# Weight sums of the seven-product feed-forward input: GpSimd additions replaced by accumulating DMAs, with all sums turned to pure sums

## The chip, the cores and the metric

The kernel runs on one core of a Trainium2 chip. The core has a matrix engine (TensorE, PE in the profile), a vector engine (VectorE, DVE), a scalar engine (ScalarE, ACT), a general engine (GpSimd, POOL) and a queue engine (SyncE, SP), each with its own instruction stream, and 16 DMA engines that serve all queues. The metric is the device time of one execution in microseconds; lower is better. Times given are medians of several runs; the profile is of one further execution.

## What is computed

A two-layer transformer-like backbone over 512 latent tokens of width 1024 with 256 context tokens, all in float32. Layer 0 mixes tokens by windowed attention, layer 1 by a gated chunk mixer; each is followed by a gated feed-forward block, and it is the input half of that block that this case is about:

```python
def swiglu(h, w_in, w_out):
    gate, up = jnp.split(h @ w_in, 2, axis=-1)
    return (jax.nn.silu(gate) * up) @ w_out
...
        x = x + g_ml * rmsnorm(y_l, norm_g[i, 1])
        f_l = swiglu(modulate(rmsnorm(x, norm_g[i, 2]), sh_fl, sc_fl), ffn_w_in[i], ffn_w_out[i])
        x = x + g_fl * rmsnorm(f_l, norm_g[i, 3])
```

Here `h` is 512 x 1024, `w_in` is 1024 x 5632 and `w_out` 2816 x 1024.

## The kernel before

**Precision.** Every float32 matrix product is made of three products of reduced-precision parts: each operand is split into a high part (a cast on ScalarE, `high`, line 217) and a low part (the operand minus its high part on VectorE, `low`, line 220), and TensorE adds high x high, high x low and low x high (`mm3`, `product`).

**The weight stream.** All weights lie in DRAM as 88 units of 128 partitions x 2048 floats (1 MB). `Stream.fetch` loads one into one of two `w_raw` buffers with a DMA issued on SP's queue. SP runs ahead of the compute engines and is held only by the semaphores of what it overwrites.

**The feed-forward input.** For layer 0 the units are 10 to 31 (`u0 = 10`), for layer 1 they are 55 to 76; unit n of a layer (n = 0 to 21) has 128 gate columns and the 128 matching up columns. Units 0 and 1 are done in the plain way (`head`). Units 2 to 21 are done by a Winograd form of Strassen's scheme: activations and weights are cut in 2 x 2 quarters (activations: half of the 1024 inputs by half of the 512 tokens; weights: half of the inputs by gate or up, B11, B12, B21, B22) and the four quarter results come from seven quarter products instead of eight. The price is sums of quarters:

- on the activation side S1 to S4, made once per layer on VectorE (`first_half`, `sum_a`), and split into high and low parts (`sum_high`, `sum_low`);
- on the weight side, for every unit, T1 = B12 - B11, T3 = B22 - B12, T2 = T3 + B11, T4 = B21 - T2. They are made by four GpSimd instructions (`diff`, line 1389) out of the raw unit into a tile named T of 128 x 2048 floats, from a pool named `big` with two buffers. The order in the tile is T1, T2, T3, T4, 512 floats each.

`part_high` and `part_low` then split four things per unit: B11 (tile `x`), T1 with T2 (part 1, `w_hi` and `w_lo` from T), the raw second half B21 with B22 (part 2, from `w_raw`), and T3 with T4 (part 3, from T). `product(n, i)` does one of the seven products: 4 slices x 3 matmuls of 128 x 128 by 256 columns (line 1432). Products 5 and 6 read part 1, products 2 and 3 part 2, products 7 and 4 part 3; product 4 of a unit is done in the step of the next unit. `keep`, `up1`, `up2` and `gate1` on ScalarE and VectorE combine the quarter results out of PSUM, `silu` and `gates` finish the activations.

**What sets the order.** `rest` (line 1495 on) writes a plan: `at(time, step, ...)` notes a step with a planned time, T = 10.08 us per unit, with b the start of a unit. `run_plan` issues the steps sorted: a step whose name stands in the list `ORDER` goes by its rank there, any other by its planned time behind them. The order on each engine's queue is the order of issue; the times themselves are not kept on the chip, where an instruction starts when its engine reaches it and its semaphores are there. In the plan `diff` of unit n + 1 stands at b + 0.02 to b + 3.9, its four `part_high` at b + 2.1, 5, 6.6 and 8.9, and the fetch of unit n + 2 at b + 9.1. `prepare` plans the first sums of a layer (unit 2) inside the end of the stage before, beside `head` and the activation sums.

Beside this the loop loads one modulation row of the next stage in 512 KB chunks on SP's queue (`fetch_chunk`, 8 per layer), adds them up on VectorE (`add_chunk`), and clears its accumulator once per layer with a memset on POOL (`Ada.start`, line 351).

Of the kernel before, what the change touches and what calls it, by code (L numbers as in the profile page):

```python
# [11 lines left out]
ALU = mybir.AluOpType  # L12
# [4 lines left out]
KC = D // P  # L17
# [141 lines left out]
f0sum_high_S1 f0head_3_1 wfetch_13 f0part_low_2_2 f0sum_low_S2 f0head_3_2 f0sum_low_S1 f0sum_high_S3 f0part_low_2_1  # L159
# [39 lines left out]
f1head_3_1 f1sum_high_S3 wfetch_58 f1sum_high_S1 f1head_3_2 f1sum_low_S1 f1sum_low_S2 f1part_low_2_3 f1sum_low_S3  # L199
# [4 lines left out]
def backbone_kernel(ctx: ExitStack, tc: tile.TileContext, a, out):  # L204
    nc = tc.nc
# [7 lines left out]
    def dma(dst, src):  # L213
        nc.sync.dma_start(out=dst, in_=src)
# [36 lines left out]
    def big(name):  # L251
        return base.tile([P, 2 * D], F32, name=name, tag="big", bufs=2)
# [1018 lines left out]
    class FFN:  # L1271
# [77 lines left out]
        def sum_a(self, name, c):  # L1349

            if c.t == 2 and name in ("S3", "S2"):
                self.sums[name] = self.sum_tile(vec if name == "S3" else stage32)
            s1, s2, s3, s4 = (self.sums[n][:, :, (c.t - 2) * P:(c.t - 1) * P] if n in self.sums else None
                              for n in ("S1", "S2", "S3", "S4"))
            a21, a22 = (c.pt[:, z * 512:(z + 1) * 512].rearrange("p (k s) -> p k s", k=4) for z in range(2))
            out, in0, in1, op = {"S3": (s3, s1, a21, ALU.subtract), "S2": (s2, a22, s3, ALU.subtract),
                                 "S1": (s1, s2, s1, ALU.add), "S4": (s4, s4, s2, ALU.subtract)}[name]
            nc.vector.tensor_tensor(out=out, in0=in0, in1=in1, op=op)
# [21 lines left out]

        def diff(self, n, i):
            if i == 1:
                self.T[n] = big("T")
            T = {j: self.T[n][:, o * 512:(o + 1) * 512].rearrange("p (k m) -> p k m", k=4)
                 for j, o in ((1, 0), (2, 1), (3, 2), (4, 3))}
            q = lambda b: self.quarter(n, b)
            x, y, op = {1: lambda: (q("B12"), q("B11"), ALU.subtract), 3: lambda: (q("B22"), q("B12"), ALU.subtract),
                        2: lambda: (T[3], q("B11"), ALU.add), 4: lambda: (q("B21"), T[2], ALU.subtract)}[i]()
            nc.gpsimd.tensor_tensor(out=T[i], in0=x, in1=y, op=op)  # L1389
# [51 lines left out]
        def up2(self, n):  # L1441
            c = self.c[n]
            nc.vector.tensor_tensor(out=c[:, 768:], in0=self.ps[n, 0], in1=c[:, 256:512], op=ALU.add)  # L1443
# [17 lines left out]
        def prepare(self, ch):  # L1461
# [29 lines left out]
        def rest(self, nxt_of, head, **kw):  # L1491
# [3 lines left out]
            for n in range(2, NFF):  # L1495
# [353 lines left out]
```

## Time and profile before

| what | value |
|---|---|
| median of 3 runs | 1141.66 us (1139.63 to 1144.7) |
| profiled execution, span from first to last instruction | 1138.5 us |
| TensorE busy | 1121.0 us, 98% |
| VectorE busy | 879.6 us, 77% |
| ScalarE busy | 565.4 us, 50% |
| POOL busy | 488.3 us, 43% |
| DMA queue of SP | 157.04 MB, 37.6% of the 16 engines' span |
| feed-forward input loops | about 304 to 505 and 808 to 1010 us |

The page gives the span of the profiled execution only; the timed runs are other executions and contain what lies ahead of the first and behind the last instruction. In the rows, a group is given as line, engine, operation, output <- inputs, count, busy time in us, mean ns of one, and the idle time of the engine just ahead of it with what ended that idle time. In a list of windows the columns are the window, its length, busy time (and number of instructions) of PE, PEld, DVE, ACT and POOL, the granted TensorE clock, the busy share of the DMA engines and GB/s. Matmuls are pipelined, so one matmul's own duration is longer than the distance from it to the next.

### The profile page before, as it was taken

To read this page: it belongs to the slowest core of one execution; us is meant where nothing else is said; L and a number is where in the kernel's file an instruction comes from. 1 tells how busy PE (TensorE), PEld (TensorE's weight loads), DVE (VectorE), ACT (ScalarE), POOL (GpSimd) and SP (SyncE) were. 2 spreads that over 40 slices of the span, in tenths; PEclk is the share of its full clock that TensorE was granted. 3 is DMA by queue.
4 is the path that set the end of the run, shared out by engine and by line. 5 is a ranking of instruction groups with operands and counts; after the bars stand their busy time and mean duration, and the time that the engine had idled before them with its cause. 6 is when DMAs were issued, how large, how long until landed. Compare 5 with 4: busy or idle time off the path is not lost.

```text
span 1138.5 us, 18345 instructions
## 1 busy us (share of the span) xinstructions
PE 1121.0 (98%) x7358; PEld 998.8 (88%) x7358; DVE 879.6 (77%) x1140; ACT 565.4 (50%) x983; POOL 488.3 (43%) x341
## 2 busy tenths in 40 slices
PE   8999999999999999999999999999999999999997
PEld 5789887768999999998888888888999999998886
DVE  6688988958988989889865768747989899953325
ACT  6357768656554455543324545345545555533322
POOL 2357475515677767730001313006577676700000
PEclk9999999999999999999999999999999999999999
DMA  9732232233134233368753265331142333323221
GB/s 370 278 137 103 102 112 75 75 148 111 57 131 149 95 136 140 130 222 320 290 185 111 87 216 194 111 114 39 66 176 96 136 140 130 130 90 133 75 74 74
DMA packets 25881, 158.21 MB, mean 139 GB/s; under 512 B 3386, under 2 KB 3642, under 8 KB 9540
## 3 DMA queue, kind: packets, MB, share of 16 engines
q1 hardware_dynamic: 25796, 157.04, 37.6%
q8 instruction: 57, 0.93, 0.3%
q14 instruction: 28, 0.23, 0.1%
HBM read 154.94 MB, written 2.10 MB: 138 GB/s over the span
## 4 chain that ended last, share of the span: by engine, by line
PE 87%; DVE 6%; DMA 2%; issue 2%; ACT 2%; POOL 0%; SPq 0%; DVEq 0%; POOLq 0%; ACTq 0%
PE f L1432 33%; PE y L272 27%; PE v L272 3%; PE o_ps L931 2%; PE pT_ps L911 2%; DMA ada<-in_ada 2%; PE s_ps L877 1%; PE u L1674 1%; PE u L1676 1%; PE u L1675 1%; PE s_ps L878 1%; PE q_ps L264 1%; PE q_ps L266 1%; PE q_ps L265 1%; DVE w_lo L220 1%
## 5 line engine op out<-in xcount | busy, mean ns | idle before, releaser
L272 PE MATMUL y<-w_hi,st 128*128 128x512 f32 x928 | 251.4, 389 | 0.0
L220 DVE TENSOR_TENSOR w_lo<-w_raw,w_hi 128x1024 fp32r<-128x1024 f32 (+1 forms) x109 | 151.5, 1391 | 100.6 <-ACT w_hi L217 100.6
L217 ACT CAST w_hi<-w_raw 128x1024 fp32r<-128x1024 f32 x122 | 127.8, 1052 | 179.1 <-PE y L272 123.7
L272 PEld LDWEIGHTS y<-w_hi,st 128*128 128x128 f32 x928 | 173.8, 188 | 36.1
L1389 POOL TENSOR_TENSOR T<-w_raw 128x512 f32<-128x512 f32 x80 | 139.1, 1759 | 111.2 <-DMA w_raw<-in_w 79.3
L1432 PE MATMUL f<-H,w_hi 128*128 128x256 f32 x960 | 178.2, 283 | 2.5 <-DVE fc L1443 2.5
L1432 PEld LDWEIGHTS f<-H,w_hi 128*128 128x128 f32 x960 | 150.1, 192 | 3.4 <-DVE fc L1443 2.9
L245 POOL TENSOR_TENSOR ry<-ry,mhalf 128x1 f32<-128x1 f32 x16 | 9.2, 576 | 327.1 <-DVE ry L242 164.2
L220 DVE TENSOR_TENSOR w_lo<-T,w_hi 128x1024 fp32r<-128x1024 f32 x80 | 143.4, 1793 | 4.4 <-ACT w_hi L217 4.4
L272 PE MATMUL y<-w_lo,st 128*128 128x512 f32 x464 | 144.2, 389 | 0.0
L1432 PE MATMUL f<-H,w_lo 128*128 128x256 f32 x480 | 135.7, 283 | 0.0
L1432 PE MATMUL f<-S,w_hi 128*128 128x256 f32 x640 | 120.0, 285 | 0.3 <-ACT fc L1439 0.3
L217 ACT CAST w_hi<-T 128x1024 fp32r<-128x1024 f32 x80 | 83.6, 1046 | 55.0 <-PE f L1432 29.7
L1439 ACT COPY fc<-f 128x256 f32<-128x256 f32 x120 | 44.8, 373 | 122.5 <-PE f L1432 120.0
L272 PEld LDWEIGHTS y<-w_lo,st 128*128 128x128 f32 x464 | 87.0, 188 | 18.0
L1432 PEld LDWEIGHTS f<-S,w_hi 128*128 128x128 f32 x640 | 99.5, 192 | 0.9 <-ACT fc L1439 0.5
L360 DVE SCALAR_TENSOR_TENSOR acc<-ada_raw,sc,acc 128x1024 f32<-128x1024 f32 x64 | 84.9, 1326 | 10.8 <-DMA ada_raw<-in_ada 8.1
L1432 PEld LDWEIGHTS f<-H,w_lo 128*128 128x128 f32 x480 | 92.1, 192 | 0.0
L1432 PE MATMUL f<-S,w_lo 128*128 128x256 f32 x320 | 90.7, 284 | 0.5 <-DVE w_lo L220 0.5
L1389 POOL TENSOR_TENSOR T<-w_raw,T 128x512 f32<-128x512 f32 x40 | 82.8, 2070 | 3.1
L905 POOL TENSOR_SCALAR p<-p,st 128x512 f32<-128x512 f32 (+1 forms) x64 | 55.7, 885 | 44.3 <-DVE st L901 21.6
L1389 POOL TENSOR_TENSOR T<-T,w_raw 128x512 f32<-128x512 f32 x40 | 69.0, 1726 | 3.1
(238 smaller groups left out, 2524.4 us busy)
## 6 DMA issues: line engine op xcount, KB each, us to landing
w_raw<-in_w SPq DMA_DIRECT2D x87, 1024.0 KB, 4.9
ada_raw<-in_ada SPq DMA_DIRECT2D x32, 1024.0 KB, 6.1
ada<-in_ada SPq DMA_DIRECT2D x8, 1024.0 KB, 9.4
ada_k<-in_ada SPq DMA_DIRECT2D x16, 512.0 KB, 5.7
row<-in_norm_g SPq DMA_DIRECT2D x7, 512.0 KB, 5.5
xin<-in_x SPq DMA_DIRECT2D x4, 512.0 KB, 7.6
x<-in_x SPq DMA_DIRECT2D x4, 512.0 KB, 6.2
out<-x SPq DMA_DIRECT2D x3, 512.0 KB, 2.6
```

Of the source, the lines that this page charges most:

```text
L217: nc.scalar.copy(out=hi, in_=src)
L220: (eng or nc.vector).tensor_tensor(out=lo, in0=src, in1=hi.bitcast(F32), op=ALU.subtract)
L264: nc.tensor.matmul(dst, lh, rh, start=first, stop=False)
L265: nc.tensor.matmul(dst, lh, rl, start=False, stop=False)
L272: nc.tensor.matmul(dst, l, w[:, n * 512:(n + 1) * 512], start=first and i == 0, stop=last and i == 2)
L360: nc.vector.scalar_tensor_tensor(out=ac, in0=w, scalar=sc[:, k:k + 1], in1=ac, op0=ALU.mult, op1=ALU.add)
L905: nc.gpsimd.tensor_scalar(out=p, in0=p, scalar1=self.st[:, 12 + j:13 + j], scalar2=1.0, op0=ALU.mult, op1=ALU.mult)
L911: nc.tensor.transpose(ps[:, j * P:(j + 1) * P], self.probs[j][:, i * P:(i + 1) * P], ident)
L931: nc.tensor.matmul(self.o[z * HD:(z + 1) * HD, c], v, pt[:, c], start=i < 2, stop=i >= self.nb - 2, tile_position=(0, z * HD), skip_group_ ...
L1389: nc.gpsimd.tensor_tensor(out=T[i], in0=x, in1=y, op=op)
L1432: nc.tensor.matmul(dst, l[:, w], r[:, k, :], start=first and k == 0 and j == 0, stop=k == 3 and j == 2, skip_group_check=True)
L1439: nc.scalar.copy(out=self.c[n][:, i * 256:(i + 1) * 256], in_=self.ps[n, 1 if i == 1 else 0])
```

## The change

The four weight sums of units 3 to 21 of both layers are no longer made by `diff`. In their place:

- `sums_start(n)` takes the T tile and issues four plain loads from DRAM on SP's queue, quarter by quarter: T1 <- B12, T2 <- B11, T3 <- B12, T4 <- B21. A quarter has rows of 128 floats (512 bytes) in DRAM. It is planned two units ahead, at b + 1.2; for unit 3 it stands in `ORDER` behind the fetch of unit 3.
- `sums_add(n, i)` issues DMAs on POOL's queue that add to what is there: for i = 0 T1 += B11 and T3 += B22 from DRAM, for i = 1 T2 += T3, for i = 2 T4 += T2, the latter two from SBUF to SBUF. Each is cut into two halves of 64 partitions, so a unit has 4 + 2 + 2 of them, 128 KB each. They are planned one unit ahead, at b - 6, b - 3.5 and b - 1.
- Signs: all four weight sums are now sums (T1 = B12 + B11, T3 = B22 + B12, T2 = T3 + B11, T4 = B21 + T2). To match, S2 and S4 change sign on VectorE (S2 by one two-operation instruction in place of a subtraction), and `up2` and `up1` subtract the product.
- `diff` remains for unit 2 of each layer, with additions.

The raw fetch of every unit remains, for B11 and for B21 with B22.

```diff
             a21, a22 = (c.pt[:, z * 512:(z + 1) * 512].rearrange("p (k s) -> p k s", k=4) for z in range(2))
-            out, in0, in1, op = {"S3": (s3, s1, a21, ALU.subtract), "S2": (s2, a22, s3, ALU.subtract),
-                                 "S1": (s1, s2, s1, ALU.add), "S4": (s4, s4, s2, ALU.subtract)}[name]
+            if name == "S2":
+                nc.vector.scalar_tensor_tensor(out=s2, in0=s3, scalar=-1.0, in1=a22, op0=ALU.mult, op1=ALU.subtract)
+                return
+            out, in0, in1, op = {"S3": (s3, s1, a21, ALU.subtract), "S1": (s1, s2, s1, ALU.add),
+                                 "S4": (s4, s4, s2, ALU.add)}[name]
             nc.vector.tensor_tensor(out=out, in0=in0, in1=in1, op=op)
...
+        def sums_start(self, n):
+
+            T, w = self.new_T(n), a["w"][self.u0 + n].rearrange("p (k z m) -> p k z m", k=KC, z=2)
+            for j, k, z in ((1, 0, 1), (2, 0, 0), (3, 0, 1), (4, 4, 0)):
+                dma(T[j], w[:, k:k + 4, z, :])
+
+        def sums_add(self, n, i):
+
+            T, w = self.t_parts(n), a["w"][self.u0 + n].rearrange("p (k z m) -> p k z m", k=KC, z=2)
+            flat = {j: self.T[n][:, (j - 1) * 512:j * 512] for j in (2, 3, 4)}
+            for h in range(2):
+                p = slice(64 * h, 64 * h + 64)
+                if i == 0:
+                    nc.gpsimd.dma_start(out=T[1][p], in_=w[p, 0:4, 0, :], accum_op=ALU.add)
+                    nc.gpsimd.dma_start(out=T[3][p], in_=w[p, 4:, 1, :], accum_op=ALU.add)
+                else:
+                    j = 2 * i
+                    nc.gpsimd.dma_start(out=flat[j][p], in_=flat[{2: 3, 4: 2}[j]][p], accum_op=ALU.add)
...
         def diff(self, n, i):
...
-            x, y, op = {1: lambda: (q("B12"), q("B11"), ALU.subtract), 3: lambda: (q("B22"), q("B12"), ALU.subtract),
-                        2: lambda: (T[3], q("B11"), ALU.add), 4: lambda: (q("B21"), T[2], ALU.subtract)}[i]()
-            nc.gpsimd.tensor_tensor(out=T[i], in0=x, in1=y, op=op)
+            x, y = {1: lambda: (q("B12"), q("B11")), 3: lambda: (q("B22"), q("B12")),
+                    2: lambda: (T[3], q("B11")), 4: lambda: (q("B21"), T[2])}[i]()
+            nc.gpsimd.tensor_tensor(out=T[i], in0=x, in1=y, op=ALU.add)
...
-            nc.vector.tensor_tensor(out=c[:, 768:], in0=self.ps[n, 0], in1=c[:, 256:512], op=ALU.add)
+            nc.vector.tensor_tensor(out=c[:, 768:], in0=c[:, 256:512], in1=self.ps[n, 0], op=ALU.subtract)
...
-            nc.vector.tensor_tensor(out=c, in0=self.ps[n, 1], in1=c, op=ALU.add)
+            nc.vector.tensor_tensor(out=c, in0=self.ps[n, 1], in1=c, op=ALU.subtract)
...
+            at(33, self.sums_start, 3)
...
                 if n < last:
-                    for i, j in enumerate((1, 3, 2, 4)):
-                        at(b + .02 + 1.28 * i, self.diff, n + 1, j)
+                    for i in range(3):
+                        at(b - 6 + 2.5 * i, self.sums_add, n + 1, i)
...
                 at(b + 9.1, ws.fetch, u0 + n + 2 if n < last - 1 else f2 + n - last + 1)
+                if n < last - 1:
+                    at(b + 1.2, self.sums_start, n + 2)
```

More of the change, by code (lines that the diff above doesn't have):

```diff
@@ L158 @@
 f0sum_a_S3#2 f0sum_a_S1 f0sum_a_S2#2 f0sum_a_S4#2 f0head_2_2 f0head_3_0 f0sum_high_S4 f0sum_a_S1#2 f0sum_high_S2
-f0sum_high_S1 f0head_3_1 wfetch_13 f0part_low_2_2 f0sum_low_S2 f0head_3_2 f0sum_low_S1 f0sum_high_S3 f0part_low_2_1
+f0sum_high_S1 f0head_3_1 wfetch_13 f0sums_start_3 f0part_low_2_2 f0sum_low_S2 f0head_3_2 f0sum_low_S1 f0sum_high_S3 f0part_low_2_1
 f0sum_low_S4 f0part_low_2_3 f0sum_low_S3 whigh_43_0 work_9_0 work_10_0 wlow_43_0 c0square_y#2 whigh_43_1 c0gain_y#2
@@ L198 @@
 f1part_high_2_3 f1head_2_2 f1sum_high_S4 f1sum_a_S1#2 f1part_low_2_1 f1head_3_0 f1sum_low_S4 f1part_low_2_2
-f1head_3_1 f1sum_high_S3 wfetch_58 f1sum_high_S1 f1head_3_2 f1sum_low_S1 f1sum_low_S2 f1part_low_2_3 f1sum_low_S3
+f1head_3_1 f1sum_high_S3 wfetch_58 f1sums_start_3 f1sum_high_S1 f1head_3_2 f1sum_low_S1 f1sum_low_S2 f1part_low_2_3 f1sum_low_S3
 """.split()
@@ L1379, in quarter, with new_T, t_parts @@
             return ws.raws[self.u0 + n].rearrange("p (k z m) -> p k z m", k=KC, z=2)[:, 4 * i:4 * i + 4, z, :]
+        def sums_start(self, n):
[13 more added lines that the diff above has]
+                    nc.gpsimd.dma_start(out=flat[j][p], in_=flat[{2: 3, 4: 2}[j]][p], accum_op=ALU.add)
+        def new_T(self, n):
+            self.T[n] = big("T")
+            return self.t_parts(n)
+        def t_parts(self, n):
+            return {j: self.T[n][:, o * 512:(o + 1) * 512].rearrange("p (k m) -> p k m", k=4)
+                    for j, o in ((1, 0), (2, 1), (3, 2), (4, 3))}
         def diff(self, n, i):
             if i == 1:
-                self.T[n] = big("T")
-            T = {j: self.T[n][:, o * 512:(o + 1) * 512].rearrange("p (k m) -> p k m", k=4)
-                 for j, o in ((1, 0), (2, 1), (3, 2), (4, 3))}
+                self.new_T(n)
+            T = self.t_parts(n)
             q = lambda b: self.quarter(n, b)
-            x, y, op = {1: lambda: (q("B12"), q("B11"), ALU.subtract), 3: lambda: (q("B22"), q("B12"), ALU.subtract),
-                        2: lambda: (T[3], q("B11"), ALU.add), 4: lambda: (q("B21"), T[2], ALU.subtract)}[i]()
-            nc.gpsimd.tensor_tensor(out=T[i], in0=x, in1=y, op=op)
+            x, y = {1: lambda: (q("B12"), q("B11")), 3: lambda: (q("B22"), q("B12")),
+                    2: lambda: (T[3], q("B11")), 4: lambda: (q("B21"), T[2])}[i]()
+            nc.gpsimd.tensor_tensor(out=T[i], in0=x, in1=y, op=ALU.add)
         def source(self, n, i):
```

## The prediction

> **What bounds the kernel now.** I read the head of the page, then the chain that ended last in order of time, then the busy time of windows inside the two feed-forward loops, then who waited for whom on TensorE.
>
> ```profile
> span 1138.5 us, 18345 instructions
> PE 1121.0 (98%) x7358; PEld 998.8 (88%) x7358; DVE 879.6 (77%) x1140; ACT 565.4 (50%) x983; POOL 488.3 (43%) x341
> L1389 POOL TENSOR_TENSOR T<-w_raw 128x512 f32<-128x512 f32 x80 | 139.1, 1759 | 111.2 <-DMA w_raw<-in_w 79.3
> L1389 POOL TENSOR_TENSOR T<-w_raw,T 128x512 f32<-128x512 f32 x40 | 82.8, 2070 | 3.1
> L1389 POOL TENSOR_TENSOR T<-T,w_raw 128x512 f32<-128x512 f32 x40 | 69.0, 1726 | 3.1
> L220 DVE TENSOR_TENSOR w_lo<-T,w_hi 128x1024 fp32r<-128x1024 f32 x80 | 143.4, 1793 | 4.4 <-ACT w_hi L217 4.4
> ```
> ```profile
> 316.80 172.80 PE f L1432 x1428
> 821.39 174.50 PE f L1432 x1452
> ```
> ```profile
> 384.00:424.00 40.00, 40.00 (x333) 39.91 (x332) 35.99 (x35) 20.24 (x36) 29.08 (x17) 1.00 0.36 132
> 888.00:928.00 40.00, 40.00 (x336) 40.00 (x335) 37.16 (x35) 20.82 (x36) 28.98 (x17) 1.00 0.37 133
> ```
> ```profile
> PE f L1432 <- DVE fc L1443: 1.4, 1, 1.4
> PE f L1432 <- DVE w_lo L220: 0.5, 1, 0.5
> ...
> PE f L1432 <- ACT fc L1439: 0.3, 1, 0.3
> ...
> PE f L1432 <- DVE fc L1443: 1.1, 1, 1.1
> PE fa L266 <- DVE H L220: 0.9, 1, 0.9
> ```
>
> The second fence is the chain: start, length, what. In the second layer 1452 matmuls of the seven products stand in a row in 174.50 us, 120.2 ns each, with nothing between them. A step (one column block, 84 matmuls: 7 products, 4 slices, 3 matmuls) therefore takes 84 x 0.1202 = 10.1 us (I use the planner's 10.08). The windows (columns: PE, PEld, DVE, ACT, POOL busy, clock, DMA share, GB/s) say the same: TensorE busy 40.00 of 40.00 at clock 1.00. The POOL work that the change removes is 139.1 + 82.8 + 69.0 = 290.9 us, but its finished sums are never what the last fence names: those are all of TensorE's waits from 264 to 330, 480 to 530 and 780 to 830 us, 1.4 + 0.5 + 0.3 + 1.1 + 0.9 = 4.2 us. So **the most that a perfect cover could gain is about 4.2 us**, 0.4%.
>
> **What goes away, and its price.** Of 160 POOL sums, the 8 for unit 2 of each layer are split 4 and 4 and stay; 152 go, 38 units' worth. Removing them shortens no chain by itself. It also frees VectorE: the low part of the T halves takes 1793 ns in the mean beside POOL and 1.23 us in the row of 380.72 below, so about 0.56 us x 76 = 43 us of VectorE, hidden under TensorE but for the 4.2 us. The turned signs (four sums per token block and the two `up` steps on VectorE) keep one instruction for one of the same size: nothing, and less than 1 us per layer if the cover were gone, since they are some dozen instructions.
>
> **What is added, per unit.** On SP's queue 4 plain loads of 256 KB in 512-byte rows (1.05 MB), behind a wait until the T buffer of two units earlier is read. On POOL's queue 8 accumulating DMAs of 128 KB: four (T1 += B11, T3 += B22, each in two partition halves), then two that wait for T3, then two that wait for T2. POOL now computes nothing here, but its queue is in order, and each wait holds what follows.
>
> ```profile
> 379.64 1.04 ACT L217 CAST w_hi<-T 128x1024 fp32r<-128x1024 f32 x1
> 383.72 1.05 ACT L217 CAST w_hi<-T 128x1024 fp32r<-128x1024 f32 x1 [1.51 <-PE f L1432]
> 380.72 1.23 DVE L220 TENSOR_TENSOR w_lo<-T,w_hi 128x1024 fp32r<-128x1024 f32 x1 [0.24 <-ACT w_hi L217]
> 382.67 1.52 DVE L220 TENSOR_TENSOR w_lo<-w_raw,w_hi 128x1024 fp32r<-128x1024 f32 x1
> 387.71 2.31 DVE L220 TENSOR_TENSOR w_lo<-T,w_hi 128x1024 fp32r<-128x1024 f32 x1
> 390.10 3.38 POOL L1389 TENSOR_TENSOR T<-w_raw 128x512 f32<-128x512 f32 x2 [1.16 <-DVE w_lo L220]
> 395.80 2.16 POOL L1389 TENSOR_TENSOR T<-w_raw,T 128x512 f32<-128x512 f32 x1
> 386.44 0.40 PE L1432 MATMUL f<-S,w_hi 128*128 128x256 f32 x2
> 393.72 0.40 PE L1432 MATMUL f<-H,w_hi 128*128 128x256 f32 x2
> 388.35 0.62 ACT L217 CAST x<-w_raw 128x512 fp32r<-128x512 f32 x1
> 384.25 0.33 SPq L214 DMA_DIRECT2D w_raw<-in_w  x1
> ```
> ```profile
> w_raw<-in_w SPq DMA_DIRECT2D x87, 1024.0 KB, 4.9
> out<-x SPq DMA_DIRECT2D x3, 512.0 KB, 2.6
> cc<-in_cc SPq DMA_DIRECT2D x1, 8.0 KB, 1.8
> L351 POOL MEMSET acc<- 128x1024 f32 x10 | 9.5, 955 | 15.5 <-PE f L1432 15.5
> ```
>
> No accumulating DMA and no DMA issued from POOL is in this trace, so two costs are bounded from rows. **Issue on POOL, g:** at least the 0.33 us that SP takes to issue a load, at most POOL's 2.16 us for one sum. I take 0.95 us, the memset: like the writing of descriptors it reads no operand. **Landing, L:** at least the 1.8 us of the 8 KB load, at most the 4.9 us of a 1 MB one. The rate comes from the windows: 132 GB/s at share 0.36 is about 365 GB/s at full share. An accumulating DMA of 131 KB must read both its operand and its destination, 0.262 MB, 0.72 us; another queue's loads run beside it for much of the step, so I double that: L = 1.8 + 1.44 = 3.24 us.
>
> From these, three limits on a step:
>
> (a) *POOL's queue.* The halves overlap: four issues (4g), T3's second half lands (L), its T2 issue (g), lands (L), its T4 issue (g). The round is 6g + 2L = 5.7 + 6.5 = **12.2 us**. Ends: 6 x 0.33 + 2 x 1.8 = 5.6 and 6 x 2.16 + 2 x 4.9 = 22.8.
>
> (b) *The 16 DMA engines.* Now 0.36 x 10.08 = 3.63 us of a step; the loads add 1.05 MB / 365 = 2.87; the adds 2.10 MB / 365 = 5.75 with both reads, half of it if the second read costs nothing. Sum **12.25 us**, or 9.4. If the 512-byte rows go at half the rate (unshown), the loads cost 5.75 and the adds 2.87 + 5.75 = 8.62, in all 18.0.
> In the Trainium skill, "Collectives: The Full Stack", section "The bandwidth ceiling: the fold count and why AG ≠ RS ≠ AR", an add in the DMA engines runs at half a copy's rate because of the second source read. By it the 12.25 stands and the 9.4 falls; no row here shows an add, so I keep both.
>
> (c) *The two T buffers.* T is free when its second low part ends, 387.71 + 2.31 = 390.02. The load of the unit two later lands 4.9 later (w_raw's row, same bytes), T4 after 6g + 3L = 15.4, cast and low part take 1.05 + 1.23: 22.6 us per two steps, 11.3 a step. SP is held there too: the raw fetch, issued now at 384.25 when the raw low part is done (382.67 + 1.52), comes behind the wait, after 390.02 and four issues of 0.33, 391.3. Both loads, 2.1 MB, take 5.75 + 1.8 and land near 398.0 to 398.9; the cast that reads the fetch comes one step after 388.35, at 398.4. Just covered; if not, 0.5 us once per layer. Behind that wait on SP stands one 512 KB chunk of the next modulation row every second step, and behind POOL's waits only the next unit's adds and one memset per layer.
>
> **Where the stall lands.** The first late T: the T12 half of the unit is cast two steps after 379.64, at 399.8. Now T2 is ready by 395.80, where POOL goes on to T4, 4 us ahead. With the change T2 lands 390.02 + 4.9 + (5g + 2L = 11.2) = 406.1, 6.3 late. Its low part ends now at 380.72 + 1.23 = 381.95 and TensorE reads it at 386.44: 4.5 us in hand. The T34 half is cast two steps after 383.72, at 403.9, and T4 lands at 390.02 + 4.9 + 15.4 = 410.3, 6.4 late, with 393.72 - 390.02 = 3.7 in hand. ScalarE is blocked in order meanwhile, and the copies that free PSUM are queued behind it, so what isn't in hand reaches TensorE: about 3 us the first time. After that the slack is spent and each step costs the excess of the slowest limit, 12.25 - 10.08 = 2.17 us.
>
> **Sum.** Units 4 to 21 of a layer: 3 + 17 x 2.17 = 39.9; two layers 79.8. Span 1138.5 + 79.8 = 1218.3. The page gives only the profiled span; the median of the runs, 1141.66, lies 3.2 above it. 1218.3 + 3.2 = **1221 us**, 7% slower.
>
> **Rivals.** *Hidden* (25%): g near SP's 0.33 and adds at copy rate give 5.6, 9.4 and (4.9 + 6 x 0.33 + 3 x 1.8 + 2.28) / 2 = 7.3 us, all within 10.08. Then 1141.7 less at most 4.2: 1137.5 to 1141.7. For it: every cost is unmeasured, and POOL's 43% becomes nearly idle. Against it: at the middle values all three limits come out above the step.
>
> *The adds land without a fight* (12%): L is the 2.6 us of the 512 KB store, the round 5.7 + 5.2 = 10.9; 3 + 17 x 0.82 = 17 per layer, 1176 us. It needs the second read to be cheap too.
> In the Trainium skill, "DMA: Bandwidth & Descriptors", section "Anatomy of one DMA — SWDGE (gpsimd) path", such a DMA takes 2.0 us plus its bytes at 436 GB/s, estimated 2.6 us for 0.26 MB, which is this case.
>
> *The halves don't overlap* (17%): if the waits are on the whole T tile, the round is 8g + 2L = 14.1, 4.0 over; 3 + 17 x 4.0 = 71, 1284 us. That the steps name disjoint partitions speaks against it.
>
> *Short rows halve the DMA rate* (7%): 18.0 us, 3 + 17 x 7.9 = 137 per layer, 1416 us.
>
> *Faster beyond the cover* (3%): VectorE's freed 43 us would have to shorten TensorE by more than 5.7 us, and its waits are 4.2.
>
> *That the change doesn't move the work:* POOL keeps the queue of all the sums, so it can stay the pacing engine while shown as idle; that is limit (a).
>
> **Chances.** 36% for the forecast, the others as given. A change of this kernel can be told from none beyond about 0.5%, 5.7 us (the three runs span 5.1). Slower: 36 + 12 + 17 + 7 = 72%; within: 25%; faster: 3%. The forecast's own range, from the 1176 to the 1284 us case and some spread beyond, is 1165 to 1310. With the hidden case and only the 18 us case left out: 1137 to 1310.
>
> **What would show it.** In windows inside the loops TensorE's busy share falls to about 0.83 (10.08 / 12.25) with the clock at 1.00; TensorE's and ScalarE's waits name POOL's DMAs or T; the matmul chain breaks once a step. If (a) is right, POOL's waits on T add to two landings a step; if (b), the DMA share is near 1; if (c), SP waits on the low part each step and then POOL on the load. DMA traffic should rise by 38 units x about 2 MB of writes. If TensorE stays at 40 of 40, the landings were shorter than bounded here and the prediction is wrong.

## The result, and the profile after

The changed kernel takes 1691.97 us in the median of 4 runs (1688.81 to 1699.42), the kernel before 1140.7 (1139.63 to 1144.7): a ratio of 1.483, interval 1.480 to 1.486. The forecast was 1221 us with a range to 1310. The direction was right; the loss is seven times as large as forecast, 551 us where some 80 were worked out.

The head of the page of the changed kernel, its 40 slices, its DMA queues and its chain by engine:

```profile
span 1697.7 us, 19325 instructions
PE 1204.7 (71%) x7358; PEld 1073.2 (63%) x7358; DVE 786.7 (46%) x1140; ACT 565.6 (33%) x983; POOL 491.7 (29%) x493
...
PE   8999999643544554558999999754454454356998
...
PEclk9999999867767766778999999976776776777999
DMA  9422232667666657668832542457676666665321
...
q1 hardware_dynamic: 106052, 196.90, 34.1%
q0 software_dynamic: 53504, 39.87, 20.0%
...
PE 37%; issue 37%; POOL 15%; DMA 4%; DVE 4%; ACT 1%; SPq 0%; POOLq 0%; DVEq 0%; ACTq 0%
```

The two holes in the row of PE are the two feed-forward input loops. The DMA engines are about two thirds busy in them, not full, and the clock is below full. In the chain, 37% is "issue": time in which the engine waited for nothing that the profile shows. Two windows in the first loop (window, length, PE, PEld, DVE, ACT, POOL, clock, DMA share, GB/s), where TensorE was busy 40.00 of 40.00 before:

```profile
344.00:384.00 40.00, 21.93 (x148) 21.71 (x149) 11.41 (x15) 10.30 (x18) 12.86 (x14) 0.69 0.65 130
384.00:424.00 40.00, 14.25 (x106) 13.82 (x104) 7.85 (x10) 5.18 (x10) 11.98 (x13) 0.73 0.70 154
```

Who waited for whom (us in total, times, longest):

```profile
PE f L1461 <- ACT fc L1468: 474.8, 40, 18.8
...
POOL T L1398 <- issue: 316.6, 71, 10.4
...
POOL T L1401 <- DMA T<-in_w: 113.5, 39, 8.2
POOL T L1397 <- issue: 111.2, 38, 4.5
POOL T L1401 <- DMA T<-T: 87.1, 59, 5.4
...
ACT w_hi L217 <- DMA T<-T: 531.0, 53, 20.7
```

TensorE waits 474.8 us for ScalarE's copies out of PSUM, about once per unit. The copies are not slow: they are queued behind the cast of T, which waits for POOL's last add. ScalarE's timeline shows the pair, the cast and the copy behind it, and TensorE's the start that follows:

```profile
401.78 1.04 ACT L217 CAST w_hi<-T 128x1024 fp32r<-128x1024 f32 x1 [17.73 <-DMA T<-T]
402.73 0.36 ACT L1468 COPY fc<-f 128x256 f32<-128x256 f32 x1
```
```profile
403.15 0.80 PE L1461 MATMUL f<-s,w_hi 128*128 128x256 f32 x2 [16.57 <-ACT fc L1468]
...
405.88 0.47 PE L1461 MATMUL f<-H,w_hi 128*128 128x256 f32 x2
...
407.38 1.60 PE L1461 MATMUL f<-H,x 128*128 128x256 f32 x12
408.82 0.40 PE L1461 MATMUL f<-S,w_hi 128*128 128x256 f32 x2
```

Windows of 2 us after the next pause, which ends at 425.75 (columns as above, the clock is the third from the end):

```profile
426.00:428.00 2.00, 2.00 (x10) 2.00 (x11) 2.00 (x3) 0.65 (x1) 0.35 (x1) 0.50 1.06 115
428.00:430.00 2.00, 2.00 (x12) 2.00 (x11) 0.15 (x1) 1.04 (x1) 0.00 (x0) 0.52 0.13 13
```

After the pause of 16.57 us the 12 matmuls of the first product take 2.73 us (403.15 to 405.88), 0.23 each; the 12 from 407.38 to 408.82 take 1.44, 0.12 each, as before. After the next pause, of 10.94 us, the granted clock is 0.50 and 0.52, and the slow stretch lasts 4.0 us (425.75 to 429.76 in TensorE's timeline, 18 matmuls, 0.22 each). Over the 38 long pauses (8.8 us and more) it lasts 2.7 to 5.9 us, some 4 in the mean, half of which is lost; so a pause costs its length and some 2 us more. TensorE's busy time rises by 1204.7 - 1121.0 = 83.7 us for the same 7358 matmuls, and the slow stretches are an estimated 38 x 2 = 76 of them. Together with the 474.8 us of waiting, the 83.7 make 558.5 of the 559.2 us by which the span grew: **TensorE stands still for T**.

Why T is late stands in POOL's timeline. One unit, from the first add of one to the first add of the next (line 1397: T1 += B11, 1398: T3 += B22, 1401: T2 += T3 and T4 += T2):

```profile
402.54 1.22 POOL L1397 DMA_DIRECT2D T<-in_w  x1
406.44 1.01 POOL L1398 DMA_DIRECT2D T<-in_w  x1 [2.68 <-issue]
410.08 1.02 POOL L1397 DMA_DIRECT2D T<-in_w  x1 [2.64 <-issue]
415.05 1.01 POOL L1398 DMA_DIRECT2D T<-in_w  x1 [3.94 <-issue]
415.67 1.27 POOL L1401 DMA_DIRECT2D T<-T  x1
420.94 1.65 POOL L1401 DMA_DIRECT2D T<-T  x2 [4.01 <-DMA T<-in_w]
424.48 0.82 POOL L1401 DMA_DIRECT2D T<-T  x1 [1.89 <-DMA T<-T]
425.14 1.22 POOL L1397 DMA_DIRECT2D T<-in_w  x1
```

The round takes 22.6 us where limit (a) had 12.2; it is the shortest of the six rounds from 349 to 501 us, the longest of which takes 29.1. The first four adds wait for nothing of one another, yet start 3.9, 3.6 and 5.0 us apart: about one landing each (medians of the adds below, from the list of DMA issues: KB each, then us to landing). From the first to the fourth start it is 12.5 us, where the prediction had three issues, 2.85; the rest of the round is 10.1 us, where it had 9.3.

```profile
T<-in_w POOLq DMA_DIRECT2D x152, 128.0 KB, 3.5
T<-T POOLq DMA_DIRECT2D x152, 128.0 KB, 3.2
```

### The profile page after: what moved, and what is told of

Its sections match the earlier page's. It is cut to its first block, busy times and chain, and to the rows that moved or that the text cites. A ratio compares the mean times of both kernels' runs of the same rounds, so it can differ in the third digit from the quotient of the medians.

```text
span 1697.7 us, 19325 instructions
## 1 busy us (share of the span) xinstructions
PE 1204.7 (71%) x7358; PEld 1073.2 (63%) x7358; DVE 786.7 (46%) x1140; ACT 565.6 (33%) x983; POOL 491.7 (29%) x493
## 3 DMA queue, kind: packets, MB, share of 16 engines
q0 software_dynamic: 53504, 39.87, 20.0%
## 4 chain that ended last, share of the span: by engine, by line
PE 37%; issue 37%; POOL 15%; DMA 4%; DVE 4%; ACT 1%; SPq 0%; POOLq 0%; DVEq 0%; ACTq 0%
PE y L272 18%; POOL T L1401 6%; POOL T L1397 4%; POOL T L1398 4%; PE v L272 2%; DMA T<-T 2%; PE o_ps L931 1%; PE f L1461 1%; PE pT_ps L911 1%; DMA ada_raw<-in_ada 1%; PE s_ps L877 1%; DMA T<-in_w 1%; PE u L1706 1%; PE u L1708 1%; PE u L1707 1%
## 5 line engine op out<-in xcount | busy, mean ns | idle before, releaser
L1461 PE MATMUL f<-H,w_hi 128*128 128x256 f32 x960 | 212.6, 320 | 240.4 <-ACT fc L1468 240.0
L220 DVE TENSOR_TENSOR w_lo<-T,w_hi 128x1024 fp32r<-128x1024 f32 x80 | 97.7, 1221 | 521.0 <-ACT w_hi L217 520.9
L1461 PEld LDWEIGHTS f<-H,w_hi 128*128 128x128 f32 x960 | 178.3, 227 | 244.9 <-ACT fc L1468 243.9
L1461 PE MATMUL f<-s,w_hi 128*128 128x256 f32 x320 | 80.9, 352 | 221.8 <-ACT fc L1468 221.8
L1461 PEld LDWEIGHTS f<-s,w_hi 128*128 128x128 f32 x320 | 65.8, 252 | 225.4 <-ACT fc L1468 225.4
L1401 POOL DMA_DIRECT2D T<-T x152 | 140.8, 937 | 201.7 <-DMA T<-in_w 113.5
L1398 POOL DMA_DIRECT2D T<-in_w x76 | 77.3, 1017 | 345.2 <-issue 316.6
L220 DVE TENSOR_TENSOR w_lo<-w_raw,w_hi 128x1024 fp32r<-128x1024 f32 (+1 forms) x109 | 132.4, 1216 | 96.6 <-ACT w_hi L217 96.6
L1461 PE MATMUL f<-H,w_lo 128*128 128x256 f32 x480 | 150.6, 314 | 0.0
L1397 POOL DMA_DIRECT2D T<-in_w x76 | 84.5, 1112 | 118.1 <-issue 111.2
L1461 PEld LDWEIGHTS f<-S,w_hi 128*128 128x128 f32 x640 | 101.5, 195 | 14.1 <-ACT fc L1468 13.6
L1461 PEld LDWEIGHTS f<-H,w_lo 128*128 128x128 f32 x480 | 108.4, 226 | 0.0
```

Of the source, the lines that this page charges most:

```text
L220: (eng or nc.vector).tensor_tensor(out=lo, in0=src, in1=hi.bitcast(F32), op=ALU.subtract)
L1397: nc.gpsimd.dma_start(out=T[1][p], in_=w[p, 0:4, 0, :], accum_op=ALU.add)
L1398: nc.gpsimd.dma_start(out=T[3][p], in_=w[p, 4:, 1, :], accum_op=ALU.add)
L1401: nc.gpsimd.dma_start(out=flat[j][p], in_=flat[{2: 3, 4: 2}[j]][p], accum_op=ALU.add)
L1461: nc.tensor.matmul(dst, l[:, w], r[:, k, :], start=first and k == 0 and j == 0, stop=k == 3 and j == 2, skip_group_check=True)
```

## The experiments

**The theories.** *Descriptor space:* the kernel sets `dynamic_dma_scratch_size=1024`, the space for the descriptors of DMAs issued by POOL; an add from DRAM with 512-byte rows has so many of them that the next must wait until it has drained, and the profile can't name that wait. *Short rows:* the 512-byte rows make the DMA engines slow. *Landings:* the chain load, T1 and T3, T2, T4 on two T buffers is too long whatever else is done. *Loads and their order:* the added loads, or the raw fetch held behind them on SP, cost the time without any adds by DMA. *Signs:* the turned signs cost something. Unless said otherwise a time is that of one execution; the kernel before took 1139.3 to 1143.4 us beside them.

**1. More descriptor space** (paid for by one buffer of `o_sb` and a shared place for `m`):

```diff
-            self.half = att_p.tile([HD, 512], F32, name="o_sb", tag="o_sb", bufs=2)
+            self.half = att_p.tile([HD, 512], F32, name="o_sb", tag="o_sb", bufs=1)
...
-        ms_[g] = gp.tile([P, SEQ], F32, name="m", tag="m", bufs=1)
+        ms_[g] = base.tile([P, SEQ], F32, name="m", tag="junk", bufs=1)
...
-    nc = _bacc.Bacc("TRN2", target_bir_lowering=False, num_devices=1, dynamic_dma_scratch_size=1024)
+    nc = _bacc.Bacc("TRN2", target_bir_lowering=False, num_devices=1, dynamic_dma_scratch_size=3072)
```

> The changed kernel with three times the space for the descriptors of POOL's DMAs (3072 bytes a partition instead of 1024), paid for by one buffer of the attention stage's o_sb and by putting the gated mixer's small tile m where the squares' junk lies. Theory ring (POOL's adds from DRAM stand one behind another because the space for descriptors holds not even two of them; 111.2 + 316.6 = 428 us of POOL's idle time in front of them has no releaser, 11.3 us a unit): this idle time falls under 60 us, the round of 22.6 us falls to what the next limit allows. By the queues' shares of the changed kernel that next limit is the DMA engines: 340 us of POOL's queue over 38 units is 8.9 us, the loads 4.0, the rest 3.6, 16.5 us a step: about 1141 + 38 x 6.4 = 1385 us. Theory engines (the 16 DMA engines already pace the step, and the idle time without a releaser is only their backlog): within 3% of 1692 us. Theory landing (the waits on what landed set the round, 113.5 + 87.1 us, 5.3 a unit): they grow to take the place, time above 1600 us.

1366.6 us: 325 of the 551 us are gone. The same with 2048 bytes:

> As the run with 3072 bytes of descriptor space (1366.6 us), with 2048. Theory ring: between it and the change's 1692 us; POOL's idle time in front of the adds from DRAM that no releaser explains, 428 us at 1024 and about 1 at 3072, lies between, 100 to 200 us, and the time at 1420 to 1520 us. Theory layout (not the space but the moved tiles made the gain): the same as 1366.6 within 1%.

1407.6 us, somewhat below what was expected. The row of the T3 adds at 1024, 2048 and 3072 bytes (count | busy, mean ns | idle time ahead, and what ended most of it):

```profile
L1398 POOL DMA_DIRECT2D T<-in_w x76 | 77.3, 1017 | 345.2 <-issue 316.6
```
```profile
L1398 POOL DMA_DIRECT2D T<-in_w x76 | 95.2, 1252 | 91.1 <-issue 82.7
```
```profile
L1398 POOL DMA_DIRECT2D T<-in_w x76 | 124.4, 1733 | 10.0 <-DMA T<-in_w 8.5 <-issue 1.0
```

The nameless idle time shrinks with the space, 316.6 to 82.7 to 1.0, and the time with it, 1692 to 1408 to 1367. The adds that POOL issues are the same in all three. The last two have the same moved tiles and still differ, so the tiles alone don't explain the gain.

**2. Longer rows**, at the old 1024 bytes: the four quarters are laid out once more in DRAM, so that each is one row of 2 KB per partition and an add from DRAM has 64 rows instead of 256.

```diff
-                dma(T[j], w[:, k:k + 4, z, :])
+                dma(self.T[n][:, (j - 1) * 512:j * 512], w[:, q * 512:(q + 1) * 512])
...
-                    nc.gpsimd.dma_start(out=T[1][p], in_=w[p, 0:4, 0, :], accum_op=ALU.add)
-                    nc.gpsimd.dma_start(out=T[3][p], in_=w[p, 4:, 1, :], accum_op=ALU.add)
+                    nc.gpsimd.dma_start(out=flat[1][p], in_=w[p, 0:512], accum_op=ALU.add)
+                    nc.gpsimd.dma_start(out=flat[3][p], in_=w[p, 1536:2048], accum_op=ALU.add)
```

> The changed kernel with its quarters laid out a second time in DRAM so that each quarter has one row of 2 KB per partition instead of four of 512 bytes; the same bytes, a quarter as many packets in the loads and in the adds from DRAM; descriptor space 1024 bytes as in the change. Theory ring: an add from DRAM now takes a quarter of the space, so seven fit, and the idle time without a releaser (428 us) falls under 60 us. Theory engines: packets of POOL's queue fall from 53504 to about 24000 and its engine time from 340 to under 200 us. Both lead to about 12.5 us a step, 1141 + 38 x 2.4 = 1232 us; read against the run with only the larger space they tell apart what the space and what the short rows cost. Theory landing: above 1500 us, since no landing is saved.

1377.8 us. POOL's waits ahead of the adds now have names, at the same descriptor space and with none of the other edits of experiment 1:

```profile
POOL T L1402 <- DMA T<-in_wq: 177.1, 70, 6.7
POOL T L1402 <- DMA T<-T: 167.8, 71, 7.6
```

**3. Both together** (the edits of 1 and 2).

> Both: 2 KB rows and 3072 bytes of descriptor space. Theory ring: with 2 KB rows the space is no longer short, so the same time as with 2 KB rows alone within 1%, about 1232 us. If the space still binds with 2 KB rows: faster than that by over 3%. Theory engines: as with 2 KB rows alone.

1377.0 us. With 2 KB rows more space gives no more, so the space was no longer short there: what the two unrelated ways relieve is one thing. The rest, some 230 us, is something else.

**4. The loads of the change, sums by GpSimd** (four additions in place, planned in the unit before their use as `diff` was, no DMA from POOL):

```diff
-            for h in range(2):
-                p = slice(64 * h, 64 * h + 64)
...
+            T = self.t_parts(n)
+            for j, x in (((1, "B11"), (3, "B22")), ((2, 3),), ((4, 2),))[i]:
+                nc.gpsimd.tensor_tensor(out=T[j], in0=T[j], in1=self.quarter(n, x) if i == 0 else T[x], op=ALU.add)
...
-                        at(b - 6 + 2.5 * i, self.sums_add, n + 1, i)
+                        at(b + .02 + 1.9 * i, self.sums_add, n + 1, i)
```

> The loads of the change stay (four quarters of 512-byte rows per unit into T, on SP's queue, two units ahead, with the wait for the T buffer in front of the raw fetch), but the sums are made in place by four GpSimd additions per unit, as many as before the change, and no DMA is issued from POOL. This tells the cost of the loads, of SP's wait and of the two T buffers by themselves. Theories ring and engines: hidden, 1141 to 1150 us, TensorE busy 40 of 40 us in the loops. Theory buffers (the loads and the T buffers alone are too slow, limit (c) of the prediction): over 1170 us, with SP's waits on the low part in every step and GpSimd waiting for the loads.

1195.7 us; GpSimd now waits for the raw fetch, which SP issues only behind the T loads:

```profile
POOL T L1394 <- DMA w_raw<-in_w: 131.0, 19, 16.7
```

**5. The same with the raw fetch issued ahead of the T loads:**

```diff
-                at(b + 9.1, ws.fetch, u0 + n + 2 if n < last - 1 else f2 + n - last + 1)
+                at(b + (1.1 if n < last - 1 else 9.1), ws.fetch, u0 + n + 2 if n < last - 1 else f2 + n - last + 1)
```

> As the run with the change's loads and GpSimd's additions in place (1195.7 us), but in SP's queue the raw fetch of a unit stands ahead of the loads into T and of their wait for the T buffer instead of behind them. Theory SP order (the 56 us of that run come from the raw fetch held behind SP's wait; GpSimd's waits for the raw unit were 131 us): GpSimd's waits for the raw unit fall to 80 us or less, time 1141 to 1155 us. Theory buffers (the two T buffers and the landing of the loads set it): within 1% of 1196 us, with GpSimd's waits moved to the loads of T.

1143.6 us, the time of the kernel before within what can be told, with TensorE busy throughout:

```profile
384.00:424.00 40.00, 40.00 (x333) 39.90 (x332) 35.04 (x34) 19.89 (x36) 28.24 (x17) 1.00 0.75 232
```

So the added 40 MB of loads, their 512-byte rows and the two T buffers are free in this order as long as no DMA adds; only their place ahead of the raw fetch cost, 52 us, because these additions read the raw unit.

**6. The signs alone**, on the kernel before (the lines of S2, S4, `up1`, `up2` and `diff` from the change, nothing of its DMAs):

```diff
+            if name == "S2":
+                nc.vector.scalar_tensor_tensor(out=s2, in0=s3, scalar=-1.0, in1=a22, op0=ALU.mult, op1=ALU.subtract)
+                return
...
-            nc.vector.tensor_tensor(out=c, in0=self.ps[n, 1], in1=c, op=ALU.add)
+            nc.vector.tensor_tensor(out=c, in0=self.ps[n, 1], in1=c, op=ALU.subtract)
```

> Only the turned signs of the change: the four weight sums stay on GpSimd as pure sums, S2, S4, up1 and up2 as in the change, no loads and no adds by DMA. All theories: the same as before, 1137 to 1143 us, ratio 1.000 within 0.003. If it is slower by more, the signs have a price that the prediction put at nothing.

1140.03 us (10 runs) against 1143.21 (13 runs), ratio 0.998, interval 0.9965 to 0.9998: no cost.

**7. The adds by DMA in the best form that was at hand:** 3072 bytes of space, one load of 1 MB with 8 KB rows for all of T, four adds over all 128 partitions in place of eight halves, T3 first, the raw fetch first.

```diff
+            dma(self.T[n], a["wt"][self.layer * NFF + n])
...
+            w, T = a["wa"][self.layer * NFF + n], self.T[n]
+            for o, src in (((1024, w[:, 512:]), (0, w[:, 0:512])), ((512, T[:, 1024:1536]),), ((1536, T[:, 512:1024]),))[i]:
+                nc.gpsimd.dma_start(out=T[:, o:o + 512], in_=src, accum_op=ALU.add)
```

> The DMA version with every price cut that the runs so far name: 3072 bytes of descriptor space, one 1 MB load into T with 8 KB rows from a copy of the weights laid out for it, four adds of 128 partitions instead of eight of 64 (T3 first), 2 KB rows, and the raw fetch ahead of the loads on SP. Theory engines (the DMA engines' time is what is left): loads 2.9, adds 6.8 by the queue's share with 2 KB rows, rest 3.6, 13.3 us a step: 1141 + 38 x 3.2 = 1263 us, with a DMA share in the loops above 0.95. Theory landing (the three landings in a row, 5.1 + 3 x (1 + 4) + 2.3 over two steps, 11.2 us): 1141 + 38 x 1.1 = 1183 us, DMA share below 0.95. Neither theory expects it at or below 1141 us.

1345.1 us: both expectations missed. Under this load the 1 MB load landed in 8.3 us and the adds from DRAM in 6.4, so one T buffer's cycle stayed long with half as many adds. This kernel also has the raw fetch first, which experiments 9 to 11 show to cost 60 to 62 us beside DMA adds; the same with the fetch behind wasn't run, so 1345 us need not be the best of this form.

**8. Adds without their bytes:** experiment 3 with each add moving 32 of its 512 columns, so that the rest of the sums is left out.

```diff
-                    nc.gpsimd.dma_start(out=flat[1][p], in_=w[p, 0:512], accum_op=ALU.add)
+                    nc.gpsimd.dma_start(out=flat[1][p][:, 0:32], in_=w[p, 0:32], accum_op=ALU.add)
```

(and so in the other two lines that issue adds)

> As the run with 2 KB rows and 3072 bytes of descriptor space (1377.0 us), but each of the eight adds of a unit moves only 32 of its 512 columns (the rest of the four weight sums is left out): the same DMAs, waits and landings, a sixteenth of the adds' bytes. Theory load (the landings of 4 to 6 us are long because adds and loads crowd the DMA engines, share 0.84 to 0.92): the landings fall to 2 to 3 us, the share to about 0.7, time 1141 to 1180 us. Theory fixed landing (three landings in a row have a fixed length, whatever they carry): above 1300 us.

1265.8 us, between the two expectations: with a sixteenth of the bytes the kernel is still 125 us slower than before. The landings of these adds, as the list of DMA issues gives them:

```profile
T<-in_wq POOLq DMA_DIRECT2D x152, 8.0 KB, 4.1
T<-T POOLq DMA_DIRECT2D x152, 8.0 KB, 3.8
```

Against experiment 3, where adds of 128 KB landed in 6.8 and 5.5 us, a landing loses 1.7 to 2.7 us with fifteen sixteenths of the adds' bytes, and an add of 8 KB lands no sooner than one of 128 KB did in the changed kernel (3.5 and 3.2): beside the loads, a landing is mostly not its own bytes.

**9. Experiment 3 with the raw fetch first** (the edit of experiment 5):

> As the run with 2 KB rows and 3072 bytes of descriptor space (1377.0 us), with the raw fetch ahead of the loads into T in SP's queue, all bytes moved. Theory load: the order on SP is not what binds here, since T comes last anyway: within 2% of 1377. Theory SP order (as it was for GpSimd's additions, where it was worth 52 us): 1330 us or less.

1439.3 us, 62 us slower than without it: neither expectation held. The T loads now land in 6.7 us instead of 5.1, but POOL stands only 2.2 us in all in front of the adds of T1 and T3 for what was loaded; its longer waits are in front of the adds of T2 and T4 (253.1 us in all for what comes from DRAM, 189.2 in experiment 3). Why this order costs here isn't shown.

**10. Half of the adds by DMA:** experiment 9 with T2 and T4 made by GpSimd.

```diff
-                else:
-                    j = 2 * i
-                    nc.gpsimd.dma_start(out=flat[j][p], in_=flat[{2: 3, 4: 2}[j]][p], accum_op=ALU.add)
+            if i > 0:
+                j = 2 * i
+                nc.gpsimd.tensor_tensor(out=flat[j], in0=flat[j], in1=flat[{2: 3, 4: 2}[j]], op=ALU.add)
```

> As the run before with the raw fetch first, but T2 and T4 are made by two GpSimd additions per unit; only T1 and T3 are added to by DMAs from DRAM. Half the adds' bytes and one landing in place of three. Theory load: DMA time a step about 3.6 + 4.0 + 3.4 = 11 us against 10.08, so 1141 + 38 x 0.9 = 1176 us, share above 0.95. Theory landing (the chain of landings, not the engines' time): hidden, 1141 to 1150 us, TensorE busy 40 of 40.

1274.0 us: both missed again. The additions stand behind the adds for 7.2 us a unit, longer than the 5.1 us in which such an add lands in the median, and the profile names no releaser:

```profile
POOL T L1402 <- issue: 275.0, 38, 8.7
```

**11. The same with the raw fetch behind the T loads**, as in the change:

> The variant with 2 KB rows and 3072 bytes of descriptor space (1377.0 us), except that T2 and T4 are made by two GpSimd additions, so that only T1 and T3 are accumulated by DMA (four adds a unit instead of eight); the raw fetch stays behind the T loads, as in the change. Beside it stands the same with the raw fetch first: 1274.0 us. If fetching first costs here what it cost with all eight adds (1439.3 against 1377.0, 62 us), this one takes 1200 to 1230 us; if it helps with four adds, as it did with none (1143.6 against 1195.7), this one takes 1300 to 1330 us.

1214.2 us, in the first of the two ranges: fetching first costs 60 us here, as it did with eight adds (62).

**12. No chain of landings:** experiment 3, but T2 and T4 add B22 from DRAM instead of T3 and T2, so they are not the reference's sums; the same eight adds of the same size, none of which waits for another's landing.

```diff
-                    nc.gpsimd.dma_start(out=flat[j][p], in_=flat[{2: 3, 4: 2}[j]][p], accum_op=ALU.add)
+                    nc.gpsimd.dma_start(out=flat[j][p], in_=w[p, 1536:2048], accum_op=ALU.add)
```

> The variant with 2 KB rows and 3072 bytes of descriptor space (1377.0 us), except that the four adds of T2 and T4 take their operand from the DRAM copy (B22) instead of from T3 and T2: same eight adds of 128 KB, same loads, but no add waits for another add's landing (T2 and T4 are then not the sums of the reference). If the chain of landings T3 -> T2 -> T4 binds, two landings of 5 to 7 us leave the 32 us that two T buffers take for two steps: (32.6 - 12)/2 = 10.3 us a step, so 1150 to 1230 us. If the DMA engines' time binds, nothing changes: 1350 to 1400 us, DMA share 0.84 to 0.95 in the loops.

1272.4 us, 105 us less than experiment 3 and again between the two expectations. The waits of adds on adds cost those 105 us (T2 and T4 now also read DRAM instead of SBUF, which this run can't tell apart). Behind them stand the DMA engines, nearly full: their share in the four windows from 344 to 504 us is 0.98, 0.90, 0.94 and 0.98, where experiment 3 had 0.84 to 0.92. Two of them:

```profile
344.00:384.00 40.00, 30.89 (x236) 30.09 (x235) 17.22 (x23) 14.21 (x27) 22.34 (x29) 0.94 0.98 253
...
464.00:504.00 40.00, 31.82 (x213) 31.39 (x214) 18.52 (x24) 13.57 (x22) 19.30 (x24) 0.83 0.98 250
```

**All of them on one scale.** A step is 10.08 us plus the time above 1141 us shared among 38 units. The engines' time per unit is the prediction's 3.63 us, plus what SP's queue (q1) took above the kernel before's 37.6% of 1138.5 = 428.1 us, plus what POOL's queue (q0) took, each over 38. The figure of 428.1 us moves from run to run: in experiment 6, which adds no DMA, it is 438.2, so the loads are known to some 0.3 us. For experiment 1 the page has

```profile
span 1364.8 us, 19318 instructions
...
q1 hardware_dynamic: 106052, 196.90, 43.0%
q0 software_dynamic: 53504, 39.87, 22.5%
```

so (586.9 - 428.1) / 38 = 4.2 for the loads and 307.1 / 38 = 8.1 for the adds, 15.9 in all.

| kernel | us | step | loads | adds | engines in all |
|---|---|---|---|---|---|
| the change | 1692.0 | 24.6 | 4.0 | 8.9 | 16.5 |
| 2048 bytes | 1407.6 | 17.1 | 4.2 | 8.1 | 15.9 |
| 1: 3072 bytes | 1366.6 | 16.0 | 4.2 | 8.1 | 15.9 |
| 2: 2 KB rows | 1377.8 | 16.3 | 4.0 | 6.8 | 14.4 |
| 3: 2 KB rows, 3072 bytes | 1377.0 | 16.3 | 3.9 | 6.8 | 14.4 |
| 9: 3 with the raw fetch first | 1439.3 | 17.9 | 3.9 | 7.4 | 15.0 |
| 7: 8 KB rows, four adds | 1345.1 | 15.5 | 3.1 | 6.4 | 13.1 |
| 10: half of the adds, raw fetch first | 1274.0 | 13.6 | 3.4 | 3.5 | 10.5 |
| 12: no chain | 1272.4 | 13.5 | 3.5 | 6.2 | 13.4 |
| 8: 32 columns | 1265.8 | 13.4 | 3.6 | 1.2 | 8.4 |
| 11: half of the adds | 1214.2 | 12.0 | 3.6 | 3.2 | 10.5 |
| 4: adds by GpSimd, raw fetch behind | 1195.7 | 11.5 | 3.7 | 0 | 7.3 |
| 5: adds by GpSimd, raw fetch first | 1143.6 | 10.1 | 4.0 | 0 | 7.6 |

Where the engines' time equals the step, they are full or nearly so: experiment 1 (share 0.97 to 1.01 in the four windows) and experiment 12. Elsewhere the step is longer than the engines need, and a wait sets it. In the change itself 8 us of each step are such a wait. In experiment 3 waits hold the step at 16.3 us, by chance just above experiment 1's full engines; that is why 2 KB rows free 1.5 us of engine time and gain nothing.

The waits can be read in the timeline of experiment 3. SP's loads of T go out, POOL's adds follow (the wait in brackets), and the same buffer's next loads go out two steps later. Below it stands the row of all adds of T2 and T4 together:

```profile
387.72 1.87 SPq L214 DMA_DIRECT2D T<-in_wq  x4
...
393.79 1.11 POOL L1398 DMA_DIRECT2D T<-in_wq  x1
395.36 0.81 POOL L1399 DMA_DIRECT2D T<-in_wq  x1 [0.46 <-DMA T<-in_wq]
...
402.96 0.81 POOL L1402 DMA_DIRECT2D T<-T  x1 [5.14 <-DMA T<-in_wq]
...
406.57 0.81 POOL L1402 DMA_DIRECT2D T<-T  x1 [1.66 <-DMA T<-T]
409.50 0.81 POOL L1402 DMA_DIRECT2D T<-T  x1 [2.12 <-DMA T<-T]
410.03 1.11 POOL L1398 DMA_DIRECT2D T<-in_wq  x1
...
419.11 2.08 SPq L214 DMA_DIRECT2D T<-in_wq  x4
```
```profile
L1402 POOL DMA_DIRECT2D T<-T x152 | 123.2, 815 | 343.7 <-DMA T<-in_wq 189.2 <-DMA T<-T 153.5 <-issue 0.9
```

From 387.72 to 419.11 it is 31.4 us for two steps, 15.7 a step: 7.6 until the first add of T3 is out, 7.6 to the first T2, 6.5 to the last T4, and 9.6 until T4 has landed, was split and the buffer is free. POOL's own round is as long: from T1's first add at 393.79 to that of the next unit at 410.03 it is 16.2 us. In front of the adds of T2 and T4 POOL stands 343.7 us in all, 9.0 a unit; in front of those of T1 and T3 some 33. So here limit (a), with landings of 5.5 to 6.8 us, is as long as limit (c), and the runs don't tell which of the two alone would be the longer.

## Why the prediction was wrong

- *What bounds the kernel before, and what could be gained:* not contradicted, but not tested. Experiment 5, at 1143.6 us, still has GpSimd's additions, and no run takes them away with the other costs hidden. The 290.9 us of removed POOL work include the eight sums that stay; 152 of the 160 are some 276.
- *Relief of VectorE, put at nothing:* the relief came, as forecast: the low part of T went from 1793 to 1221 ns. What it is worth can't be told in a kernel whose VectorE stands waiting for T:

```profile
L220 DVE TENSOR_TENSOR w_lo<-T,w_hi 128x1024 fp32r<-128x1024 f32 x80 | 97.7, 1221 | 521.0 <-ACT w_hi L217 520.9
```

- *Signs, put at nothing:* right (experiment 6).
- *Issue g = 0.95 us and landing L = 3.24 us:* near what the changed kernel shows, in part by luck. The rows of the issues take 0.94 to 1.11 us in the mean, but where nothing holds POOL the next one starts 0.5 to 0.6 us later (415.05 and 415.67 above; 395.88 and 396.40 in experiment 3), so as a term of the round g was too long. The landings take 3.2 to 3.5 us, with the adds from DRAM going out one at a time; with more of them under way they take 4.7 to 7.7 us.
- *Limit (a), 6g + 2L = 12.2 us:* **this step failed.** It let four adds go out one behind the other. The model had no term for the space that their descriptors need; the adds from DRAM went out one landing apart, and the round was 22.6 us at its shortest and 24.6 a step by the time. Relieving that space alone, in two ways, gave back 314 to 325 of the 551 us. That the full space is what POOL waits for is inferred from how the time follows the space and from the two ways, since the profile names no releaser. Of the rest, some 230 us, this limit has its share too: in experiment 3 its round is 16.2 us, with landings of 5.5 to 6.8 us in place of 3.24. The prediction did say that POOL can stay the pacing engine while shown as idle, and so it was, at 29% busy.
- *Limit (b), 12.25 us on the DMA engines:* right in kind, undersized. The loads took 4.0 instead of 2.87 us a unit and the adds 8.9 instead of 5.75; 6.2 to 7.4 with 2 KB rows, and the loads 3.1 in one piece with rows of 8 KB (experiment 7). The rate of 365 GB/s came from windows with one stream of 8 KB rows; in a mixture it was not reached. In the change this limit was hidden under the failed one.
- *Limit (c), two T buffers at 11.3 us a step:* right in kind, undersized: 15.7 us in the cycle of experiment 3, because a landing was taken at its unloaded length. Under load the adds from DRAM land in 6.8 us (experiment 3), and even 8 KB ones in 3.8 to 4.1.
- *SP's hold on the raw fetch, "just covered":* not shown to cost in the change. Putting the fetch first, which takes the hold away, made the variants with DMA adds 60 to 62 us slower. Only where additions read the raw unit did the hold cost, 52 us, far more than the half microsecond a layer put for it.
- *How the stall reaches TensorE:* right. ScalarE's in-order queue carried it, through the PSUM copies behind the cast, once a step. The clock "at 1.00" was wrong: 0.67 to 0.80 in the twelve windows of 40 us from 304 to 784 us, with matmuls at half speed after the pauses; TensorE's busy share there was 0.51, not 0.83.
- *The rivals:* "hidden" failed with the DMA adds, and holds for the loads alone. "Short rows halve the DMA rate" gave a time nearest to the result, 1416 us, for a reason that doesn't hold: the loads' engine time is 3.9 to 4.2 us with rows of 512 bytes and of 2 KB alike. What short rows cost is descriptor space, as inferred above, and 1.3 us in the adds. "The halves don't overlap" failed: at 415.67 the first half of T2 goes out 0.6 us behind the second half of T3.
- *The range:* it bounded the price of one DMA from both sides, but not the number of DMAs that can be under way. At one at a time the prediction's own terms give 4 (g + L) = 16.8 for the first four adds and some 9 for the rest, 26 us: 36 units at (26 - 10.08) us added to 1141 make about 1710 us. That end was missing.

What stays open: why a landing beside the loads takes 4 us even for 8 KB (experiment 8), and so how the 125 us there divide between waiting in the DMA engines and waiting for completion; and whether a third T buffer would help, which wasn't tried; it would not by itself shorten POOL's round, which is as long. No variant with adds by DMA came near the kernel before; the nearest, with half of the adds, takes 1214.2 us.

## What to carry to other kernels

Before work is moved from an engine to DMAs that it issues, ask how many of them can be under way at once, and weigh the descriptors, which grow with the number of rows, against the space the kernel gives them; a price per DMA says nothing when they go out one at a time. Time in front of a DMA issue that the profile puts down to nothing was the sign of it here, and doubling the space is a cheap test. A chain of dependent DMAs should be costed with landings under the load it will itself add, and an accumulating DMA as about twice a copy.

## What the runs showed of the hardware

- **Descriptor space.** With 1024, 2048 and 3072 bytes, POOL stood in front of the T3 adds for 316.6, 82.7 and about 1 us with no releaser shown. The Trainium skill's page "DMA: Bandwidth & Descriptors", section "Terms", gives 16 bytes to a descriptor; 1024 bytes a partition are then an estimated 64 of them in each partition. How many an add takes, no run shows.
- **Adds against copies.** Per byte written, the adds took the DMA engines longer than loads: in experiment 12, 39.87 MB in 18.5% of 1270.6 us, 170 GB/s, against 39.86 MB in (44.3% of 1270.6) - 428.1 = 134.8 us, 296 GB/s. That is 0.57 of the loads' rate, near the half that the prediction's two reads give. With the 512-byte rows of experiment 1 it is 0.52, in the change 0.44.
- **TensorE after a pause.** 2.7 to 5.9 us at half speed in the change, some 4 in the mean, 0.23 against 0.12 us a matmul. The Trainium skill's page "TensorE: Matmul & The Clock Gate", section "Part 1: The HAM clock gate (the "warmup" mystery)", gives a window of some 3.4 us at half rate after an idle one; the trace agrees in kind, with stretches on both sides of that length.
- **The order of two loads has no sign of its own.** Issuing the raw fetch ahead of the T loads gained 52 us where additions read the raw unit, and lost 60 to 62 us where DMAs added.
